# A two-layer decoder step on one core: gate and value of the feed-forward, for both row groups at once, from seven half-depth products in place of eight

## The chip, the cores and the metric

The kernel runs on one core of one Trainium2 chip. A core has a matrix engine (TensorE, PE in the profile, with its weight loads listed apart as PEld), three engines for element-wise work (VectorE or DVE, ScalarE or ACT, GpSimd or POOL), a queue engine that issues transfers (SP), an on-chip memory of 128 partitions (SBUF) and an accumulator memory of eight banks (PSUM). The metric is the device time of one execution in microseconds (us). Three timed runs of the kernel before gave 1133.88, 1135.64 and 1136.44 us; the median is 1135.64 us.

## What is computed

One inference step of a two-layer decoder on 520 rows of 1024 features: a new sequence of 512 rows ("prompt") and eight single rows of other sequences ("sample"). Layer 0 mixes tokens by windowed attention, layer 1 by gated linear attention; each is followed by a layer normalisation, a gated feed-forward with a causal convolution of width 3, and another normalisation. The change concerns the feed-forward. Cut to what matters, the reference has:

```python
def conv_ffn(x, buf, w_up, conv_w, conv_b, w_down):
    T = x.shape[1]
    h = x @ w_up
    a, u = h[..., :D_FF], h[..., D_FF:]
    ap = jnp.concatenate([buf.astype(a.dtype), a], axis=1)
    c = conv_b + sum(conv_w[j] * ap[:, j:j + T] for j in range(CONV_W))
    y = (jax.nn.gelu(c, approximate=False) * u) @ w_down
    return y, ap[:, T:]
...
        xp = layer_norm(ALPHA * xp + mp, ln_mix_g[i], ln_mix_b[i])
...
        fp, cp = conv_ffn(xp, buf0, ffn_w_up[i], ffn_conv_w[i], ffn_conv_b[i], ffn_w_down[i])
...
        xp = layer_norm(ALPHA * xp + fp, ln_ffn_g[i], ln_ffn_b[i])
```

D_FF is 2816, that is 22 blocks of 128 inner features; a is called the gate and u the value. All arrays are 32-bit floats.

## The kernel before

**Rows and groups.** Activations lie transposed: features on the 128 partitions, rows along the free axis. The 520 rows are cut into group a (prompt rows 0 to 255) and group b (prompt rows 256 to 511 and the 8 sample rows, 264 in all).

**A product in three passes.** TensorE multiplies numbers of type fp32r, which hold fewer bits than a 32-bit float. So each operand is kept as a pair: a rounded part ("h": `wh` of weights, `xh` of activations) and the rest ("l": `wl`, `xl`), and a product is the sum of three passes, wh·xh, wh·xl and wl·xh (lines 198, 200 and 202). `split` makes the pairs: ScalarE rounds (line 228, for weights 167), VectorE subtracts the rounded part from the original (line 229, for weights 170). A unit of work is one 128x1024 block of weights: one 512 KB transfer into a `raw` tile, one split, and one product of 8 depth steps for each group. Where both parts of group a's activations stand side by side (`xs_a`, `hs_a`), `product2` runs wh against both in one matmul of 512 columns and wl against one of 256 (lines 221 and 222); the two halves of the result are added afterwards.

**The feed-forward.** For inner block j there are two units, gate and value. `ffn_gate` copies the gate from PSUM into `aext` (line 637), forms the convolution into `conv` (lines 642 to 644; 648 for sample rows) and applies the Gelu (line 653). `ffn_value` multiplies (line 665) and splits the result into `hh` and `hl`. The 22 blocks come in three parts of 6, 8 and 8; after each part, eight units of the down-projection (`ffn_down`) add their share to the residual `x`. From block 4 on (`WIDE`), and in the first two parts of the down-projection, group a's products have the 512-column form.

**What sets the order.** `order` lists the products: group b follows group a some four or five units behind. Code that belongs later is put off by a number of products (`spawn`, `resume`, `due`). A scheduler then places each engine's instructions; the engines run them strictly in that order and wait for one another through semaphores. Six buffers hold split weights (`wts`), and a seventh (`wx`, `EXTRA`) during the feed-forward; as group b leaves a unit, the next one not yet loaded is started. `raw` has two buffers, the accumulators `accp` four banks.

**Before the feed-forward.** `ln_end` finishes the normalisation of each group: it writes `xh` and `xl`, and later adds a bias to `x` on GpSimd, one block at a time (line 361).

Of the kernel before, what the change touches and what calls it, by code (L numbers as in the profile page):

```python
# [46 lines left out]
EXTRA = 1  # L47
XEND = 8
# [12 lines left out]

WIDE = 4
# [35 lines left out]
class Net:  # L98
# [109 lines left out]
    def product2(self, g, u, rs, rh, rl, wide):  # L208


        if rs is None or not wide:
            return self.product(g, u, rh, rl), None
        nc = self.nc
        h, l = self.w[u]
        nt = self.units[u][1]
        ps = self.acc.tile([P, 512], F32, name="accp")
        o = ps.rearrange("p (j t) -> p j t", t=2)
        for k in range(nt):
            ks = slice(k * P, (k + 1) * P)
            last = k == nt - 1  # L220
            both = lambda: nc.tensor.matmul(o, h[:, ks], in_turn(rs[:, k].rearrange("p t q j -> p t (q j)")), start=k == 0, stop=last)  # L221
            low = lambda: nc.tensor.matmul(o[:, :P], l[:, ks], in_turn(rh[:, k]), start=False, stop=False)  # L222
            for f in (low, both) if last else (both, low):
                f()
        return ps[:, :256], ps[:, 256:]
# [59 lines left out]
    def ln_end(self, g, i, last=False):  # L285
# [319 lines left out]
    def ffn_open(self, layer):  # L605
        nc = self.nc
        if EXTRA:
            self.wx, self.wx_cm = self.open(f"wts{layer}", EXTRA)
# [10 lines left out]
        t = p.tile([P, NF, NS], F32, name="baset")  # L619
# [37 lines left out]
    def ffn_value(self, g, u, layer, j, q):  # L657
        nc, n = self.nc, g.n
        ps, lo = self.product2(g, u, g.xs, g.xh, g.xl, j >= WIDE)
        h = self.fp.tile([P, NT - 256], F32, name="hprod", bufs=2)  # L660
        if lo is not None:
            nc.scalar.copy(h[:, :n], lo)
            nc.vector.tensor_tensor(h[:, :n], h[:, :n], ps, op=ALU.add)
            ps = h[:, :n]
        nc.vector.tensor_tensor(h[:, :n], g.gate[:, :n], ps, op=ALU.mult)
# [507 lines left out]
```

## Time and profile before

| | value |
|---|---|
| timed, three runs (us) | 1133.88, 1135.64, 1136.44 |
| profiled execution, span (us) | 1131.7 |
| PE busy (us, share of the span) | 1104.2, 98% |
| PEld busy | 1055.1, 93% |
| DVE busy | 777.2, 69% |
| ACT busy | 565.7, 50% |
| POOL busy | 319.3, 28% |
| instructions on PE, DVE, ACT, POOL | 8806, 1626, 1251, 591 |
| read from main memory, written | 108.67 MB, 8.47 MB |

The span is the profiled execution's own time from its first to its last instruction; the timed runs lie 2.2 to 4.7 us above it. Busy times overlap, since engines work side by side. Matmuls are pipelined: the row of one shows about 280 ns, though the next starts 112 ns later, so the pace of a product is read from start to start. In a row of the profile, "out<-in" names the tiles written and read, "x6" counts instructions, and what follows "<-" in brackets is what the engine had waited for.

### The profile page before, as it was taken

Reading aid. Unit: us, or ns where it says so; the run is one execution under the profiler, and the core shown is the slowest. Engines: PE = TensorE matmul, PEld = TensorE weight load, DVE = VectorE, ACT = ScalarE, POOL = GpSimd, SP = SyncE. Lnnn points to the kernel's source line nnn. Section 1 sums busy time; section 2 is a strip of 40 time slices with the busy share of each in tenths; the row PEclk is TensorE's granted clock in tenths of the full one; section 3 lists DMA queues with packets and bytes.
Section 4 is the critical chain, followed back from the end, with each engine's and each line's share of the span. In section 5 each row is a group of like instructions: output and inputs, shape, how many; then the busy total and the mean of one; then the engine's idle time right before and its main releaser. Section 6 shows DMA issues by size and latency. Waiting matters only on the chain.

```text
span 1131.7 us, 22912 instructions
## 1 busy us (share of the span) xinstructions
PE 1104.2 (98%) x8806; PEld 1055.1 (93%) x8806; DVE 777.2 (69%) x1626; ACT 565.7 (50%) x1251; POOL 319.3 (28%) x591
## 2 busy tenths in 40 slices
PE   8999999999999999999999999999999999999996
PEld 7997799999999999999899999899999999999995
DVE  7897579655665566568867778779756665566565
ACT  5677556534553245435455556456524553245433
POOL 4575574400110011255211100374400110001243
PEclk9999999999999999999899999999999999999998
DMA  7553023333233233242124354432333223223222
GB/s 244 150 178 96 16 75 101 105 103 121 94 105 102 93 100 106 75 134 94 57 90 145 122 178 160 139 111 94 113 98 127 94 98 109 93 96 110 76 64 76
DMA packets 53804, 122.81 MB, mean 109 GB/s; under 512 B 6808, under 2 KB 27328, under 8 KB 53696
## 3 DMA queue, kind: packets, MB, share of 16 engines
q1 hardware_dynamic: 51536, 119.47, 32.8%
q10 hardware_dynamic: 2160, 1.89, 0.5%
q8 instruction: 69, 1.13, 0.4%
q14 instruction: 39, 0.32, 0.1%
HBM read 108.67 MB, written 8.47 MB: 104 GB/s over the span
## 4 chain that ended last, share of the span: by engine, by line
PE 77%; DVE 10%; DMA 5%; ACT 3%; issue 2%; POOL 1%; SPq 0%; ACTq 0%; DVEq 0%; POOLq 0%
PE accp L198 16%; PE accp L200 16%; PE accp L202 16%; PE accp L221 15%; PE accp L222 8%; DMA vb<-dv 2%; DVE xs_a L355 1%; DVE wl L183 1%; DVE wl L170 1%; DMA raw<-in_w_up 1%; DMA qs<-hl 1%; DVE sgla L910 1%; DVE x_a L353 1%; PE pv L554 1%; ACT pr L523 1%
## 5 line engine op out<-in xcount | busy, mean ns | idle before, releaser
L170 DVE TENSOR_TENSOR wl<-raw,wh 128x1024 fp32r<-128x1024 f32 (+2 forms) x172 | 207.0, 1205 | 103.3 <-ACT wh L167 102.7
L198 PE MATMUL accp<-xh_b,wh 128*128 128x264 f32 x976 | 272.5, 279 | 1.8 <-ACT xh_b L354 1.7
L167 ACT ACTIVATE wh<-raw 128x1024 fp32r<-128x1024 f32 (+2 forms) x168 | 173.6, 1033 | 199.8 <-PE accp L200 187.3
L202 PE MATMUL accp<-xh_b,wl 128*128 128x264 f32 x976 | 270.8, 277 | 0.0
L200 PE MATMUL accp<-xl_b,wh 128*128 128x264 f32 x960 | 266.5, 278 | 0.0
L221 PE MATMUL accp<-xs_a,wh 128*128 128x512 f32 x576 | 196.3, 382 | 0.0
L198 PEld LDWEIGHTS accp<-xh_b,wh 128*128 128x128 f32 x976 | 184.8, 189 | 3.3 <-ACT xh_b L354 2.3
L202 PEld LDWEIGHTS accp<-xh_b,wl 128*128 128x128 f32 x976 | 184.5, 189 | 0.8 <-issue 0.6
L200 PEld LDWEIGHTS accp<-xl_b,wh 128*128 128x128 f32 x960 | 181.6, 189 | 2.5 <-issue 0.4
L222 PE MATMUL accp<-xs_a,wl 128*128 128x256 f32 x576 | 145.4, 273 | 0.0
L198 PE MATMUL accp<-hh_b,wh 128*128 128x264 f32 x480 | 134.2, 280 | 1.7 <-ACT hh_b L228 1.1
L200 PE MATMUL accp<-hl_b,wh 128*128 128x264 f32 x480 | 134.6, 280 | 0.3 <-DVE hl_b L594 0.2
L202 PE MATMUL accp<-hh_b,wl 128*128 128x264 f32 x480 | 133.6, 278 | 0.0
L221 PEld LDWEIGHTS accp<-xs_a,wh 128*128 128x128 f32 x576 | 109.1, 189 | 11.4
L222 PEld LDWEIGHTS accp<-xs_a,wl 128*128 128x128 f32 x576 | 110.2, 191 | 1.9
L198 PE MATMUL accp<-xs_a,wh 128*128 128x256 f32 x400 | 107.6, 284 | 1.4 <-ACT wh L167 0.6
L200 PE MATMUL accp<-xs_a,wh 128*128 128x256 f32 x384 | 103.0, 282 | 0.6 <-DVE xs_a L229 0.3
L198 PEld LDWEIGHTS accp<-hh_b,wh 128*128 128x128 f32 x480 | 91.6, 191 | 2.3 <-ACT hh_b L228 1.6
L200 PEld LDWEIGHTS accp<-hl_b,wh 128*128 128x128 f32 x480 | 91.5, 191 | 1.8 <-DVE hl_b L594 0.4
L202 PEld LDWEIGHTS accp<-hh_b,wl 128*128 128x128 f32 x480 | 91.5, 191 | 0.2
L232 POOL COPY hist<-aext 128x2 f32<-128x2 f32 x44 | 10.2, 231 | 283.7 <-DVE aext L641 277.2
L198 PEld LDWEIGHTS accp<-xs_a,wh 128*128 128x128 f32 x400 | 77.2, 194 | 2.8 <-ACT wh L167 1.0
(338 smaller groups left out, 2505.5 us busy)
## 6 DMA issues: line engine op xcount, KB each, us to landing
raw<-in_w_up SPq DMA_DIRECT2D x88, 512.0 KB, 3.4
raw<-in_w_down SPq DMA_DIRECT2D x32, 512.0 KB, 3.4
raw<-in_w_gla SPq DMA_DIRECT2D x24, 512.0 KB, 3.4
raw<-in_w_mix_o SPq DMA_DIRECT2D x16, 512.0 KB, 4.1
raw<-in_w_down SPq DMA_DIRECT2D x16, 384.0 KB, 3.0
qs<-hl SPq DMA_DIRECT2D x64, 64.0 KB, 2.2
sgla<-in_state_gla SPq DMA_DIRECT2D x16, 256.0 KB, 2.7
vb<-dv SPq DMA_DIRECT2D x16, 256.0 KB, 3.7
```

The lines of the kernel that those rows point to most:

```text
L167: nc.scalar.activation(h[:, c], r[:, c], AF.Copy)
L170: nc.vector.tensor_tensor(l[:, c], r[:, c], h[:, c].bitcast(F32), op=ALU.subtract)
L183: self.nc.vector.tensor_tensor(l, r, h.bitcast(F32), op=ALU.subtract)
L198: nc.tensor.matmul(o, h[:, ks], xh, start=k == 0, stop=False)
L200: nc.tensor.matmul(o, h[:, ks], xl, start=False, stop=False)
L202: nc.tensor.matmul(o, l[:, ks], xh, start=False, stop=not tail and k == nt - 1)
L221: both = lambda: nc.tensor.matmul(o, h[:, ks], in_turn(rs[:, k].rearrange("p t q j -> p t (q j)")), start=k == 0, stop=last)
L222: low = lambda: nc.tensor.matmul(o[:, :P], l[:, ks], in_turn(rh[:, k]), start=False, stop=False)
L353: v = nc.vector.scalar_tensor_tensor(x[:, m], x[:, m], sc(m), rp, op0=ALU.mult, op1=ALU.mult)
L355: xl = nc.vector.scalar_tensor_tensor(g.xl[:, m], parted(x[:, m]), bi(m), g.xh[:, m].bitcast(F32), op0=ALU.add, op1=ALU.subtract)
L523: nc.scalar.activation(pr[:, b, 0:P + 1], sc[:, b, 0:P + 1], AF.Exp, bias=nm[:, b:b + 1], accum_out=den[:, b:b + 1])
L554: mm = nc.tensor.matmul(pv[64 * v:64 * v + 64, b * P:(b + 1) * P], self.vtok[:, kb, 64 * v:64 * v + 64], parts[v][w][:, b], start=i == 0, ...
```

## The change

From block j = 4 on (`PAIRED`), gate and value are one unit, a pair of weight blocks (`ffn_pair`). Cut the depth of 1024 into a lower and an upper half: the gate's weights become A11 and A12, the value's A21 and A22, the rows' halves B11 and B21 for group a and B12 and B22 for group b. The four results, gate and value for a and for b, are a product of two 2x2 block matrices, eight half-depth products. Winograd's form of Strassen's algorithm needs seven, at the price of sums: of weights (s1 to s4, four additions for each pair), of rows (t1 to t4, once in each layer) and of results.

- `load_pair` fetches two blocks, adds s1 to s4 on GpSimd, and splits seven half-blocks (as three tiles of 1024 columns and one of 512) where two units had four.
- `row_sums`, called by `ln_end`, makes t1 to t4 on GpSimd; `row_sum1` writes the split of t1 over group b's `xh` and `xl` when the first pair begins.
- `half_product` is 4 depth steps of three matmuls with 256 or 264 columns. `ffn_pair` calls it seven times and combines the results on VectorE (lines 765, 768, 776, 778 and 781), ScalarE (763 and 772) and GpSimd (773 and 779). Convolution, Gelu and gate times value then run over both groups at once (lines 784 to 791).
- The 512-column form is gone everywhere, also from the first two parts of the down-projection, and so is the seventh weight buffer. A pair takes three of the six weight buffers (`COST`) and a smaller tile of its own for s4; a new pair is begun when three are free (`load_next`).
- In `order`, a pair comes once both groups are up to date, and in the first two parts of the down-projection group b follows two units behind (`DOWNLAG`).

The diff, cut to its core:

```diff
+    def load_pair(self, u):
+        nc, half = self.nc, KD * P // 2
+        src0, src1 = self.units[u][0]
+        r0 = self.raw.tile([P, KD * P], F32, name="raw")
+        r1 = self.pp.tile([P, KD * P], F32, name="raw1", bufs=2)
+        nc.sync.dma_start(out=r1, in_=src1)
+        nc.sync.dma_start(out=r0, in_=src0)
+        s = self.pp.tile([P, KD * P], F32, name="sums")
+        s4 = self.pp.tile([P, half], F32, name="sum4")
+        lo, hi = slice(0, half), slice(half, KD * P)
+        add = lambda o, x, y: nc.gpsimd.tensor_tensor(o, x, y, op=ALU.add)
+        add(s[:, lo], r1[:, lo], r1[:, hi])
+        add(s[:, hi], s[:, lo], r0[:, lo])
+        add(s4, s[:, hi], r0[:, hi])
+        add(r1[:, lo], r1[:, lo], r0[:, lo])
+        for src in (r0, s, s4, r1):
+            pool, name = (self.pp, "4") if src is s4 else (self.wts, "")
+            h, l = (pool.tile(list(src.shape), F32R, name=part + name) for part in ("wh", "wl"))
+            self.split(h, l, src)
...
+    def half_product(self, ps, w, x, n):
...
+        for k in range(KD // 2):
+            ks = slice(k * P, (k + 1) * P)
+            rh, rl = (in_turn(r[:, k, :, :n // 2]) for r in (xh, xl))
+            self.nc.tensor.matmul(o, h[:, ks], rh, start=k == 0, stop=False)
+            self.nc.tensor.matmul(o, h[:, ks], rl, start=False, stop=False)
+            self.nc.tensor.matmul(o, l[:, ks], rh, start=False, stop=k == KD // 2 - 1)
...
+    def row_sums(self, i):
...
+        for k in range(half):
+            tt(self.t1[k], a.x[:, k, 0:256], b.x[:, k, 0:256], ALU.subtract)
+        r2, r3 = (self.pp.tile([P, KD * P], F32, name="raw1", bufs=2) for _ in range(2))
+        for k in range(half):
+            self.shift(b, i, half + k)
+            tt(r2[:, 256 * k:256 * k + 256], b.x[:, half + k, 0:256], self.t1[k], ALU.add)
+        for k in range(half):
+            self.shift(b, i, k)
+        tt(wide(r3), rows(b, hi), rows(b, lo), ALU.subtract)
...
+        r4 = self.pp.tile([P, KD * P], F32, name="sums")
+        tt(wide(r4), wide(r2), rows(a, hi), ALU.subtract)
...
     def ffn_gate(self, g, u, layer, j, q):
-        ps, lo = self.product2(g, u, g.xs, g.xh, g.xl, j >= WIDE)
+        ps = self.product(g, u, g.xh, g.xl)
...
+    def ffn_pair(self, u, layer, j, q):
...
+        self.half_product(p1, W["a11"], part(a, lo), n)
+        v = t("v", bufs=2)
+        nc.gpsimd.memset(v[:, n:], 0.0)
+        nc.scalar.copy(v[:, :n], p1[:, :n])
+        self.half_product(p2, W["a12"], part(a, hi), n)
+        nc.vector.tensor_tensor(g[:, 2:2 + n], p2[:, :n], v[:, :n], op=ALU.add)
+        q6, p5 = bank(), bank()
+        self.half_product(q6, W["s2"], t2, m)
+        nc.vector.tensor_tensor(v, q6[:, :m], v, op=ALU.subtract)
+        self.half_product(p5, W["s1"], t1, m)
+        s5, h = t("s5"), t("hprod", NT)
+        y = h[:, n:]
+        nc.scalar.copy(s5, p5[:, :m])
+        nc.gpsimd.tensor_tensor(y, s5, v, op=ALU.subtract)
+        p3, p7, q4 = bank(), bank(), bank()
+        self.half_product(p3, W["s4"], part(b, hi), m)
+        nc.vector.tensor_tensor(g[:, 2 + n:], p3[:, :m], y, op=ALU.add)
+        self.half_product(p7, W["s3"], t3, m)
+        nc.vector.tensor_tensor(v, v, p7[:, :m], op=ALU.subtract)
+        nc.gpsimd.tensor_tensor(h[:, n:], v, s5, op=ALU.subtract)
+        self.half_product(q4, W["a22"], t4, n)
+        nc.vector.tensor_tensor(h[:, :n], v[:, :n], q4[:, :n], op=ALU.subtract)
...
+        nc.vector.tensor_tensor(h, c, h, op=ALU.mult)
+        self.split(a.hh[:, q], a.hl[:, q], parted(h[:, :n]))
+        self.split(b.hh[:, q], b.hl[:, q], parted(h[:, n:]))
...
     def ffn_down(self, g, u, layer, part, m):
-        ps, lo = self.product2(g, u, g.hs, g.hh, g.hl, part < 2)
+        ps = self.product(g, u, g.hh, g.hl)
...
+    def load_next(self):
+        while self.nu < len(self.units) and self.live + self.cost(self.nu) <= WSLOTS:
+            u = self.nu
+            self.nu += 1
+            self.live += self.cost(u)
```

**Inside a part, VectorE.** Before, the instructions of one block in the second part stand in this row; `aext`, `conv` and `hprod` are the gate, its convolution and the product with the value:

```order
L170 TENSOR_TENSOR wl<-raw,wh 128x1024
L648 SCALAR_TENSOR_TENSOR conv<-aext,par,base 128x8
L643 SCALAR_TENSOR_TENSOR conv<-aext,par,conv 128x256
L644 SCALAR_TENSOR_TENSOR conv<-aext,par,conv 128x256
L663 TENSOR_TENSOR hprod<-hprod,accp 128x256
L665 TENSOR_TENSOR hprod<-conv,hprod 128x256
L229 TENSOR_TENSOR hs_a<-hprod,hs_a 128x2x128
L665 TENSOR_TENSOR hprod<-conv,accp 128x264
```

Now the row reads as follows, from a pair's fifth product on to the next pair's third (`raw_4454` is the value's raw block, with s3 in it, of the pair after next; `raw` and `sums` are the gate's block and s1 with s2 of the pair behind that one):

```order
L776 TENSOR_TENSOR aext<-accp,hprod 128x264
L778 TENSOR_TENSOR v<-v,accp 128x264
L787 SCALAR_TENSOR_TENSOR conv<-aext,par,base 128x8
L781 TENSOR_TENSOR hprod<-v,accp 128x256
L251 TENSOR_TENSOR wl<-raw_4454,wh 128x1024
L785 SCALAR_TENSOR_TENSOR conv<-aext,par,conv 128x512
L786 SCALAR_TENSOR_TENSOR conv<-aext,par,conv 128x512
L251 TENSOR_TENSOR wl<-raw,wh 128x1024
L765 TENSOR_TENSOR aext<-accp,v 128x256
L791 TENSOR_TENSOR hprod<-conv,hprod 128x520
L768 TENSOR_TENSOR v<-accp,v 128x264
L251 TENSOR_TENSOR wl<-sums,wh 128x1024
```

Behind these follow the splits of `hprod` for a and b and that of `sum4` (512 columns), and the row begins anew. The result of a pair's last product (line 781), the next pair's first (765) and third (768) are now separated by weight splits of the pair to come.

**Inside a part, GpSimd.** Before, a block gave GpSimd only fills and copies of 2 or 8 columns:

```order
L634 MEMSET aext 128x2
L232 COPY nconv_p<-aext 128x2
L232 COPY nconv_s<-aext 128x8
L232 COPY aext<-hist 128x2
L232 COPY hist<-aext 128x2
```

Now each pair gives it these:

```order
L222 TENSOR_TENSOR sums<-raw_4599 128x512
L762 MEMSET v 128x8
L222 TENSOR_TENSOR sums<-sums,raw 128x512
L222 TENSOR_TENSOR raw_4599<-raw_4599,raw 128x512
L758 MEMSET aext 128x2
L773 TENSOR_TENSOR hprod<-s_4538,v 128x264
L222 TENSOR_TENSOR sum_4603<-sums,raw 128x512
L254 COPY nconv_p<-aext 128x2
L254 COPY nconv_s<-aext 128x8
L779 TENSOR_TENSOR hprod<-v,s_4538 128x264
```

Six two-operand instructions per pair are new, four of them 512 columns wide, and the fill of `aext` that a pair's line 765 waits for stands behind three of these.

**At the start of a feed-forward, GpSimd.** Before, the bias of the normalisation stands among small copies:

```order
L361 TENSOR_SCALAR x_b<-x_b,par 128x264
L232 COPY aext<-hist 128x2
L232 COPY hist<-aext 128x2
L361 TENSOR_SCALAR x_a<-x_a,par 128x256
L232 COPY nconv_p<-aext 128x2
```

Now the row sums stand between the biases, and the first two pairs' weight sums behind them (`raw_2793` and `raw_2794` hold t2 and t3, `sums` first t4, then s1 and s2):

```order
L399 TENSOR_TENSOR raw_2793<-x_b,msq 128x256
L391 TENSOR_SCALAR x_b<-x_b,par 128x264 x4
L399 TENSOR_TENSOR raw_2794<-x_b 128x1024
L399 TENSOR_TENSOR tsum<-x_b 128x32
L391 TENSOR_SCALAR x_a<-x_a,par 128x256 x4
L254 COPY hist<-aext 128x2
L399 TENSOR_TENSOR sums<-raw_2793,x_a 128x1024
L254 COPY aext<-hist 128x2
L254 COPY nconv_p<-aext 128x2
L254 COPY nconv_s<-aext 128x8
L222 TENSOR_TENSOR sums<-raw_3227 128x512
```

The first pair's sums begin only when t4 has been formed.

More of the change, by code (lines that the diff above doesn't have):

```diff
@@ L45 @@
 HIACT = 2
-EXTRA = 1
-XEND = 8
+PAIRED = 4
+COST = 3
+DOWNLAG = 2
 ACCS = 4
@@ L60 @@
 LOWS = 7
-WIDE = 4
 SPAUSE = 2
@@ L206, in product, with cost @@
         return ps[:, :g.n]
[L208 to L218, printed above, removed]
-            ks = slice(k * P, (k + 1) * P)
[L220 to L225, printed above, removed]
+    def cost(self, u):
+        return COST if isinstance(self.units[u][0], tuple) else 1
@@ L363, in load_x, with row_sum1 @@
+    def row_sum1(self):
+        nc, b, n = self.nc, self.groups[1], P
+        for k in range(KD // 2):
+            self.split(b.xh[:, k, :, :n], b.xl[:, k, :, :n], parted(self.t1[k]))
+        for r in (b.xh, b.xl):
+            r = r[:, 0:KD // 2, :, n:]
+            nc.gpsimd.tensor_scalar(r, r.bitcast(F32), -1.0, 0.0, op0=ALU.mult, op1=ALU.add)
     def load_x(self, i, m0, m1):
@@ L618, in ffn_open @@
         b = self.par[:, C_CB + layer * NF:C_CB + (layer + 1) * NF].unsqueeze(2).broadcast_to([P, NF, NS])
-        t = p.tile([P, NF, NS], F32, name="baset")
+        self.pp, self.pp_cm = self.open(f"pair{layer}")
+        s = lambda i: [P, KD // 2, 2, (256 + NS * (i < 2)) // 2]
+        self.th, self.tl = ([self.pp.tile(s(i), F32R, name=f"{n}{i}") for i in range(3)] for n in ("th", "tl"))
+        self.cp, self.cp_cm = self.open(f"chain{layer}")
+        t = self.cp.tile([P, NF, NS], F32, name="baset")
         g = nc.gpsimd
@@ L658, in ffn_value @@
         nc, n = self.nc, g.n
[L659 to L664, printed above, removed]
+        ps = self.product(g, u, g.xh, g.xl)
+        h = self.cp.tile([P, NT - 256], F32, name="hprod", bufs=2)
         nc.vector.tensor_tensor(h[:, :n], g.gate[:, :n], ps, op=ALU.mult)
@@ L1001, in order @@
             for u in range(p0, p1):
-                out.append((0, u))
+                pair = self.cost(u) > 1
                 lead = max(LAG, min(top, p0 + 2 * top - u))
@@ L1005, in order @@
                     lead = LAG - 1
[L1006 removed]
+                if pair:
+                    lead = 0
+                elif self.units[u][2] == self.ffn_down and self.units[u][3][1] < 2:
+                    lead = DOWNLAG
+                if not pair:
+                    out.append((0, u))
+                while b <= u - max(lead, 1):
                     out.append((1, b))
                     b += 1
+                if pair:
+                    out.append((2, u))
+                    b = u + 1
             out += [(1, u) for u in range(b, p1)]
         return out
[L1012 to L1025 removed]
+    def load_next(self):
+        while self.nu < len(self.units) and self.live + self.cost(self.nu) <= WSLOTS:
+            u = self.nu
+            self.nu += 1
+            self.live += self.cost(u)
+            late = self.units[u][1] and any(e < u < e + 6 for e in (*self.phases[2:4], *self.phases[5:6]))
+            self.load_unit(u, late=late)
     def run(self):
@@ L1039, in run @@
                 pre()
-                if pre != self.gla_open:
-                    for _ in range(EXTRA):
-                        self.next_unit(True)
-            self.slot += 1
-            self.resume(f(g, u, *a))
-            if i == 1:
-                x = self.extra.pop(u, False)
-                if not x or self.more(u):
-                    self.next_unit(x)
-                elif not self.extra:
-                    self.close_wx = True
-            if self.close_wx and self.fp is None:
-                self.close(self.wx_cm)
-                self.close_wx = False
+            self.slot += COST if i == 2 else 1
+            if i == 2:
+                f(u, *a)
+            else:
+                self.resume(f(self.groups[i], u, *a))
+            if i:
+                self.live -= self.cost(u)
+                self.load_next()
             self.due()
```

116 lines of the change are left out of this document (81 added, 35 removed).

## The prediction

> **What bounds the kernel now.** I read the page first: its sums, then the chain of work that ended last.
>
> ```profile
> span 1131.7 us, 22912 instructions
> PE 1104.2 (98%) x8806; PEld 1055.1 (93%) x8806; DVE 777.2 (69%) x1626; ACT 565.7 (50%) x1251; POOL 319.3 (28%) x591
> PE 77%; DVE 10%; DMA 5%; ACT 3%; issue 2%; POOL 1%; SPq 0%; ACTq 0%; DVEq 0%; POOLq 0%
> ```
>
> PE is busy 98% of the span and makes up 77% of the chain. Inside the stage that is changed it is fuller still. One inner block, in the busy times by stretch (columns: length, then PE, PEld, DVE, ACT and POOL busy with their instructions, granted clock, DMA):
>
> ```profile
> core 0: us, PE busy (x) PEld busy (x) DVE busy (x) ACT busy (x) POOL busy (x), PEclk, DMA share, GB/s
> 289.80:300.40 10.60, 10.60 (x82) 10.18 (x81) 6.82 (x14) 5.77 (x11) 1.29 (x5) 1.00 0.32 100
> ```
>
> So the stage is bound by the matrix engine at full clock, VectorE is two thirds full, and GpSimd has little to do. The pace of a product is read from start to start in the order of time on PE:
>
> ```profile
> 176.02 0.28 PE L198 MATMUL accp<-xs_a,wh 128*128 128x256 f32 x1
> ...
> 178.70 0.28 PE L198 MATMUL accp<-xs_a,wh 128*128 128x256 f32 x1
> ...
> 276.61 0.38 PE L221 MATMUL accp<-xs_a,wh 128*128 128x512 f32 x1
> ...
> 279.23 0.28 PE L198 MATMUL accp<-xh_b,wh 128*128 128x264 f32 x1
> ...
> 281.93 0.38 PE L221 MATMUL accp<-xs_a,wh 128*128 128x512 f32 x1
> ```
>
> A unit takes 2.62 us for group a in the 512-column form and 2.70 for b, 5.32 together; a block of two units 10.64. A plain product of a, the 24 matmuls from 176.02 to 178.70, takes 2.68.
>
> **PE's work.** Seven half-products replace four products: three of 256 columns (2.68 / 2 = 1.34) and four of 264 (1.35), 9.42 us. A pair saves 10.64 − 9.42 = 1.22 us, and 36 pairs (18 in each layer) 43.9. The down-projection loses the 512-column form in its first two parts: 14 depth steps x 8 units x 2 layers x (2.68 − 2.62) / 8 = +1.7. If PE stayed the bound, that would be nearly all.
>
> **VectorE's work for a pair.** Durations by form and by tile:
>
> ```profile
> L170 DVE TENSOR_TENSOR wl<-raw,wh 128x1024 fp32r<-128x1024 f32 x150 | 187.7, 1252 | 90.0 <-ACT wh L167 89.5 <-PE accp L202 0.3
> L391 DVE TENSOR_TENSOR wl<-raw,wh x2: 693/694/694, 4.3 to 7.8; 128x512 fp32r<-128x512 f32 x2
> L665 DVE TENSOR_TENSOR hprod<-conv,accp 128x264 f32<-128x264 f32 x44 | 18.9, 430 | 25.4 <-PE accp L202 25.3
> L229 DVE TENSOR_TENSOR hl_b<-hprod,hh_b 128x264 fp32r<-128x264 f32 x44 | 21.3, 485 | 1.2 <-ACT hh_b L228 1.2
> L648 DVE SCALAR_TENSOR_TENSOR conv<-aext,par,base 128x8 f32<-128x8 f32 x44 | 10.0, 227 | 0.1
> ```
>
> Weight splits: three of 1.25 and one of 512 columns, 0.69: 4.44. Five results from PSUM at 0.43: 2.15. Convolution: two of 512 columns, 0.73 each by the 0.69 row and its small surplus for a third operand (my estimate), and 0.23: 1.69. Gate times value over 520 columns: 0.70. Two splits at about 0.47: 0.94. Together 9.9 us against 6.8 before. VectorE alone would then be no faster than 9.9; instructions that follow without a wait start up to 0.1 early (169.55 + 0.48 against 169.96 below), so some 8.8 to 9.9. That is level with PE's 9.42.
>
> ScalarE rounds the same columns, 3.5 tiles at 1.06, and adds copies and activations of about 2.8, 6.5 us a pair. It is not the bound:
>
> ```profile
> L167 ACT ACTIVATE wh<-raw 128x1024 fp32r<-128x1024 f32 x150 | 158.8, 1059 | 169.2 <-PE accp L200 157.1 <-DMA raw<-in_w_mix_o 7.5 <-DMA raw<-in_w_up 1.5
> ```
>
> **What GpSimd does to VectorE.** This term decides. At the start of the first feed-forward both engines work at once; their rows in order of time, VectorE's first:
>
> ```profile
> 160.29 2.05 DVE L353 SCALAR_TENSOR_TENSOR x_a<-x_a,par,pv 128x256 f32<-128x256 f32 x5
> ...
> 169.55 0.48 DVE L355 SCALAR_TENSOR_TENSOR xs_a<-x_a,par,xs_a 128x256 fp32r<-128x256 f32 x1
> 169.96 1.75 DVE L183 TENSOR_TENSOR wl<-raw,wh 128x1024 fp32r<-128x1024 f32 x1
> 171.63 0.42 DVE L252 SCALAR_TENSOR_TENSOR x_b<-x_b,accp 128x264 f32<-128x264 f32 x1
> ```
>
> ```profile
> 157.35 4.18 POOL L306 TENSOR_TENSOR x_a<-x_a,mu 128x256 f32<-128x256 f32 x6
> 161.48 0.75 POOL L282 TENSOR_TENSOR s_b<-s_b,x_b 128x264 f32<-128x264 f32 x1
> ...
> 169.75 0.87 POOL L282 TENSOR_TENSOR s_b<-s_b,x_b 128x264 f32<-128x264 f32 x1 [1.99 <-DVE x_b L252]
> 170.59 1.73 POOL L283 TENSOR_TENSOR s_b<-s_b,sq 128x264 f32<-128x264 f32 x1
> ```
>
> The weight split at 169.96 takes 1.75 in place of 1.25, since GpSimd's addition runs until 170.62; GpSimd's next one, issued at 170.59, takes 1.73 in place of 0.75, since it waits for that split. The two take turns. The five instructions at 160.29 have one operand in PSUM and take their usual 0.41 each beside GpSimd's 0.75. So VectorE instructions with two SBUF operands exclude GpSimd's, and those with a PSUM operand do not.
>
> The Trainium skill ("SBUF — State Buffer", Who interferes with whom) says that the engines share a port pair which the first comer holds for its whole instruction; the rows agree up to 264 columns, and by this rule a 512-column addition shuts VectorE out to its end, which the low price in the second rival below would deny.
>
> How long does GpSimd hold it? Six of 256 columns take 4.18, 0.70 each; one of 176 takes 0.55:
>
> ```profile
> L623 POOL TENSOR_TENSOR base<-base,baset x2: 547/552/557, 144.0 to 751.0; 128x176 f32<-128x176 f32 x2
> L389 POOL TENSOR_SCALAR wh<-raw x2: 619/736/853, 3.7 to 6.9; 128x512 fp32r<-128x512 f32 x2
> ```
>
> (0.70 − 0.55) / 80 is 1.9 ns a column, so 512 columns with two operands cost 0.70 + 256 x 0.0019 = 1.2 us. Below stands the row with one operand, 0.74; above, twice 264 columns, 1.5. I take 1.25. A pair has four of these and two of 264 columns (0.72): 6.4 us, and 0.2 for two small copies: 6.6.
>
> VectorE's two-operand work holds the port for its columns alone, about (1.25 − 0.69) / 512 = 1.1 ns each: 3584 columns of splits, 1024 of convolution, 520 and 520: 5648 columns, 5.9 to 6.2 us. Port time per pair: 6.6 + 6.1 = 12.7. That exceeds 10.64 already. Walking one period in the order of the two engines, the port also stands idle: the fill of `aext` stands behind three additions, line 765 waits for it, and GpSimd then has nothing until line 768 gives `v`; lines 765, 768 and part of 776 and 778 pass with the port unused, about 1.1 us. A period of **13.8 us**, with PE waiting 4.4 in it, in two gaps of about 2 (banks free only once VectorE reaches lines 765, 768, 776 and 778). Bounds: 12.7 − 4 x 0.5 = 10.7 if the additions cost the one-operand row, 9.9 if they blocked nothing; above, every hold added to VectorE's 9.9, less 2.1 beside PSUM operands, 14.4, and with additions at 1.5, 15.4.
>
> **Which pairs pay it.** Two pairs' weights fit in the six buffers. In a part of eight pairs, six are computed while another pair is prepared; the last two have only down-projection blocks beside them. There, and for the two pairs in the first part, PE sets the pace, about 9.7. So 24 pairs of 36 take 13.8, and 12 take 9.7: 24 x (13.8 − 10.64) = +75.8 and 12 x (9.7 − 10.64) = −11.3.
>
> **Start of the feed-forward.** This stretch runs from the normalisation to block 4:
>
> ```profile
> 144.00:202.00 58.00, 56.98 (x492) 55.99 (x491) 48.10 (x89) 34.71 (x67) 34.92 (x50) 1.00 0.30 100
> ```
>
> Added on GpSimd: eight sums of 256 columns (5.6), two of 1024 (about 2.2 each), eight of 512 (10): 20 us on 34.9, so 55 of 58. Added on VectorE: the first two pairs' splits less the four units' they replace (8.9 − 5.0), those of t2 to t4 (3.8) and t1 (1.9): 9.6 on 48.1, so 57.7. With half of GpSimd's 20 in VectorE's way it is 68, 10 too late: **+10** in each layer, between 0 and 20. Total +20.
>
> **End of a part.** The last pair's gate and value for both groups become ready together. From its last result come gate times value, ScalarE's rounding and the subtraction, 0.7 + 0.5 + 0.5 with their waits some 3 us; the first down-projection product covers seven of its eight steps, 2.35. About 1 us each, six times: +6.
>
> Sum: 75.8 − 11.3 + 20 + 6 + 1.7 = **+92**. The profiled execution would be 1131.7 + 92 = 1224; the timed median lies 3.9 above the span, so **1228 us**. Transfers are no term: the same bytes at the 100 GB/s of the block above, over a longer stage.
>
> **Rivals.**
>
> 1. *PE stays the bound, the other engines fit in* (faster). VectorE's 8.8 to 9.9 lies beside 9.42, GpSimd's additions fall where VectorE has PSUM operands: −43.9 + 1.7 + 6, 1135.6 − 36 = **1099**; at VectorE's 9.9 for 24 pairs, −17.8 − 11.3 + 7.7, **1114**. It decides if GpSimd's holds cost VectorE under 0.9 us a pair. For it speaks PE's fullness and that ScalarE is free; against it the turns at 169.96. Chance 0.13.
>
> 2. *Port bound, but at its floor*: shorter holds, better packing, 12.6 a pair, the start 4 late. 24 x 1.96 − 11.3 + 8 + 4 + 1.7 = +49, **1185**. Chance 0.18.
>
> 3. *PE's gaps also cost clock.* In one place of this trace PE stood still for 2.6 us:
>
> ```profile
> 541.00:543.60 2.60, 0.02 (x2) 0.01 (x1) 2.60 (x9) 1.47 (x5) 0.00 (x0) 1.00 0.02 6
> 543.60:554.00 10.40, 10.32 (x35) 8.31 (x36) 7.81 (x21) 6.03 (x14) 0.00 (x0) 0.51 0.06 13
> ```
>
> The clock was then half for 10.4 us. Two gaps of 2 us in each period could do the same. Always at half, a pair would take 18.8; three quarters of the time, 9.42 / 0.625 = 15.1, so some 15.5 with the other waits: 24 x 4.86 − 11.3 + 20 + 7.7 = +133, **1269**. In the other periods the slack of 4.4 absorbs it. Chance 0.18.
>
> The Trainium skill ("TensorE: Matmul & The Clock Gate", Part 1) has the clock fall after an idle window of about 3.4 us, so gaps of 2 us would not do it and this rival would get no chance. The row above shows 2.6 us to be enough, and I go by the row.
>
> 4. *Nothing to be seen*: the steady pairs come out near 11, the gain of the other twelve making up for the rest. Chance 0.03.
>
> **How the numbers follow.** The forecast keeps 0.48. Faster by over 0.2% is rival 1, 0.13 less a little for its upper edge: 0.12. Within 0.2%, about what a measurement of this kernel can tell from no change, 0.03; slower 0.85. The range reaches over rival 2 and most of rival 3 and holds back rival 1 and the far end: 1150 to 1285.
>
> **What would show it.** In the profile after, right if: a pair in the middle of a part takes 13 to 15 us from one first product to the next; there VectorE's weight splits average 1.7 us or more and GpSimd's 512-column additions 2 us or more; PE's idle time names line 765, 768, 776 or 778 of VectorE as its releaser; the two last pairs of a part take under 10. Wrong if PE stays above 95% busy in the pairs, if the additions average under 1 us, or if the splits keep their 1.25. The start term shows as PE idle time ahead of the first pair of each layer, the clock rival as PEclk under 0.9 in the pairs' slices.

## The result, and the profile after

The changed kernel takes **1212.5 us** (median, 1212.1 to 1213.4) against 1135.3 for the kernel before on the same chip: 1.069 times as long, with a 95% interval of 1.067 to 1.070. Times are medians; one of the four executions of experiment 4, a slow one of 2824 us, is left out. The profiled execution took 1213.4 us with a span of 1211.5, 79.8 more than the 1131.7 before; the forecast was +92.

From the page of the changed kernel, its sums, the granted clock in 40 slices, and the chain that ended last:

```profile
span 1211.5 us, 24182 instructions
PE 1104.3 (91%) x9174; PEld 1063.1 (88%) x9174; DVE 957.2 (79%) x1684; ACT 598.3 (49%) x1233; POOL 614.9 (51%) x797
PEclk9999998899989999999899999998899899999898
PE 44%; DVE 28%; issue 8%; ACT 7%; POOL 6%; DMA 6%; SPq 0%; DVEq 0%; ACTq 0%; POOLq 0%
```

PE is as long busy as before although it has less to do (part of it at half clock), and its share of the chain fell from 77% to 44%, VectorE's rose from 10% to 28%. VectorE gained 180 us of busy time, GpSimd 296.

Where the 80 us lie is read from the busy times by stretch (columns as in the prediction). Of the first layer: four plain blocks, two pairs, down-projection, eight pairs, down-projection, eight pairs; of the second: the same start and the two runs of eight:

```profile
core 0: us, PE busy (x) PEld busy (x) DVE busy (x) ACT busy (x) POOL busy (x), PEclk, DMA share, GB/s
167.13:223.90 56.77, 50.21 (x391) 46.99 (x390) 48.65 (x73) 29.90 (x56) 46.07 (x56) 0.94 0.26 84
223.90:253.50 29.60, 22.59 (x171) 22.27 (x170) 25.52 (x41) 14.80 (x28) 15.42 (x24) 0.88 0.39 121
253.50:285.80 32.30, 32.30 (x291) 32.30 (x290) 19.61 (x30) 10.03 (x12) 10.64 (x10) 1.00 0.27 87
285.80:380.70 94.90, 82.42 (x675) 80.60 (x674) 86.64 (x111) 48.16 (x75) 58.37 (x67) 0.95 0.31 100
...
423.70:517.50 93.80, 79.98 (x675) 77.95 (x674) 86.51 (x110) 48.21 (x75) 55.58 (x65) 0.98 0.26 86
...
799.90:859.20 59.30, 51.93 (x391) 48.94 (x391) 49.48 (x78) 30.68 (x57) 48.06 (x59) 0.91 0.28 91
859.20:887.60 28.40, 21.96 (x170) 21.64 (x169) 23.55 (x38) 14.63 (x27) 13.28 (x21) 0.88 0.33 109
...
919.90:1014.80 94.90, 82.67 (x674) 80.80 (x673) 86.23 (x110) 48.11 (x75) 58.33 (x67) 0.95 0.30 100
1058.00:1153.50 95.50, 82.10 (x675) 80.56 (x674) 86.94 (x111) 47.99 (x75) 55.51 (x65) 0.95 0.26 83
```

The same stretch at the start of the kernel before holds 4 x 10.76 + 2 x 10.64 = 64.3 us of products, with PE standing still for 1.0:

```profile
167.00:231.30 64.30, 63.28 (x512) 61.23 (x511) 51.35 (x101) 36.15 (x73) 25.87 (x51) 1.00 0.33 105
```

In the start PE also works at a lowered clock, which the kernel before does not (1.00 above). Two pieces of it:

```profile
195.00:202.00 7.00, 5.77 (x36) 5.77 (x37) 3.70 (x6) 3.12 (x6) 7.00 (x12) 0.66 0.24 76
...
237.00:244.00 7.00, 7.00 (x48) 7.00 (x49) 4.91 (x10) 3.21 (x6) 2.59 (x7) 0.76 0.58 187
```

In the second PE has no gap and gets through 48 matmuls, where 7 us at full clock hold 65 (216 to 223).

Put against the prediction's terms (a run of eight blocks before: 8 x 10.64 = 85.1):

| term | forecast | measured |
|---|---|---|
| four runs of eight pairs | 24 x 3.16 − 8 x 0.94 = +68 | 379.1 − 340.5 = +39 |
| start and the two pairs behind it, both layers | +20 − 4 x 0.94 = +16 | 174.1 − 128.6 = +45 |
| ends of parts, down-projections | +6 + 1.7 = +8 | the rest, −4 |
| sum | +92 | +80 |

So two errors of about 30 us, of opposite sign, hide in a total that is off by 12: that the total came so close is luck.

**A steady period.** VectorE in order of time, from one line 778 to the next:

```profile
308.21 0.42 DVE L778 TENSOR_TENSOR v<-v,accp 128x264 f32<-128x264 f32 x1
308.54 0.53 DVE L787 SCALAR_TENSOR_TENSOR conv<-aext,par,base 128x8 f32<-128x8 f32 x1
...
309.33 1.77 DVE L251 TENSOR_TENSOR wl<-raw,wh 128x1024 fp32r<-128x1024 f32 x1
311.02 1.76 DVE L785 SCALAR_TENSOR_TENSOR conv<-aext,par,conv 128x512 f32<-128x512 f32 x1
312.82 1.64 DVE L786 SCALAR_TENSOR_TENSOR conv<-aext,par,conv 128x512 f32<-128x512 f32 x1
314.38 2.28 DVE L251 TENSOR_TENSOR wl<-raw,wh 128x1024 fp32r<-128x1024 f32 x1
316.59 0.41 DVE L765 TENSOR_TENSOR aext<-accp,v 128x256 f32<-128x256 f32 x1
...
321.03 0.43 DVE L776 TENSOR_TENSOR aext<-accp,hprod 128x264 f32<-128x264 f32 x1 [0.65 <-POOL hprod L773]
321.38 0.42 DVE L778 TENSOR_TENSOR v<-v,accp 128x264 f32<-128x264 f32 x1
```

and GpSimd in the same time:

```profile
307.78 1.27 POOL L222 TENSOR_TENSOR sum<-sums,raw 128x512 f32<-128x512 f32 x1
...
309.26 0.76 POOL L779 TENSOR_TENSOR hprod<-v,s 128x264 f32<-128x264 f32 x1
309.98 2.26 POOL L222 TENSOR_TENSOR sums<-raw 128x512 f32<-128x512 f32 x1
...
312.31 1.60 POOL L222 TENSOR_TENSOR sums<-sums,raw 128x512 f32<-128x512 f32 x1
313.88 1.71 POOL L222 TENSOR_TENSOR raw<-raw,raw 128x512 f32<-128x512 f32 x1
```

The period is 13.17 us. The sum at 307.78 lies beside lines 776 and 778, which have a PSUM operand: it takes 1.27 and costs VectorE only 0.3 us, in line 787 (0.53 in place of 0.23). What follows takes turns with VectorE. The split at 309.33 takes 1.77, since GpSimd's line 779 runs until 310.02. The sum at 309.98 waits for that split, which ends at 311.10, then runs to 312.24; line 785, issued at 311.02, ends 0.54 behind it; 312.31 waits for line 785 (312.78) and runs to 313.91, line 786 ends 0.55 behind it; and so on. Line 765, which frees a PSUM bank, comes only then, and PE's waits name it. In the whole period VectorE is busy for 12.5 of the 13.17 us, and for the other 0.65 it waits, ahead of line 776, for GpSimd's line 773. The largest waits of PE (engine, line, releaser: us in total, times, longest):

```profile
PE accp L245 <- DVE aext L765: 42.2, 17, 3.1
PE accp L245 <- DVE hprod L737: 13.4, 4, 4.5
PE accp L198 <- ACT wh L167: 8.1, 6, 2.3
PE accp L245 <- DVE aext L776: 7.5, 16, 1.3
```

The groups of instructions by form, for comparison with the experiments (xcount | busy us, mean ns | idle before):

```profile
L251 DVE TENSOR_TENSOR wl<-raw,wh 128x1024 fp32r<-128x1024 f32 x72 | 129.1, 1794 | 12.2 <-ACT wh L250 12.2
L785 DVE SCALAR_TENSOR_TENSOR conv<-aext,par,conv 128x512 f32<-128x512 f32 x36 | 47.7, 1326 | 0.7 <-ACT conv L784 0.7
L222 POOL TENSOR_TENSOR sums<-raw 128x512 f32<-128x512 f32 x36 | 65.9, 1832 | 54.7 <-issue 26.5 <-DVE wl L251 24.5 <-DVE tl L251 3.5
```

### The profile page after: what moved, and what is told of

Its sections match the earlier page's. It is cut to its first block, busy times and chain, and to the rows that moved or that the text cites. A ratio compares the mean times of both kernels' runs of the same rounds, so it can differ in the third digit from the quotient of the medians.

```text
span 1211.5 us, 24182 instructions
## 1 busy us (share of the span) xinstructions
PE 1104.3 (91%) x9174; PEld 1063.1 (88%) x9174; DVE 957.2 (79%) x1684; ACT 598.3 (49%) x1233; POOL 614.9 (51%) x797
## 4 chain that ended last, share of the span: by engine, by line
PE 44%; DVE 28%; issue 8%; ACT 7%; POOL 6%; DMA 6%; SPq 0%; DVEq 0%; ACTq 0%; POOLq 0%
PE accp L200 9%; PE accp L198 9%; PE accp L202 9%; DVE wl L251 4%; PE accp L245 4%; PE accp L246 3%; PE accp L247 3%; DVE conv L786 3%; DVE conv L785 3%; DMA vb<-dv 2%; ACT wh L250 2%; POOL hprod L773 2%; ACT conv L790 1%; DVE wl L170 1%; DMA raw<-in_w_qkv 1%
## 5 line engine op out<-in xcount | busy, mean ns | idle before, releaser
L245 PE MATMUL accp<-th,wh 128*128 128x264 f32 (+1 forms) x432 | 128.5, 297 | 44.4 <-DVE aext L765 42.2
L170 DVE TENSOR_TENSOR wl<-raw,wh 128x1024 fp32r<-128x1024 f32 (+3 forms) x102 | 124.8, 1227 | 22.6 <-ACT wh L167 22.0
L251 DVE TENSOR_TENSOR wl<-raw,wh 128x1024 fp32r<-128x1024 f32 x72 | 129.1, 1794 | 12.2 <-ACT wh L250 12.2
L200 PE MATMUL accp<-hs_a,wh 128*128 128x256 f32 x480 | 131.3, 277 | 0.6 <-DVE hs_a L251 0.6
L202 PE MATMUL accp<-hs_a,wl 128*128 128x256 f32 x480 | 130.8, 276 | 0.0
L198 PE MATMUL accp<-hs_a,wh 128*128 128x256 f32 x480 | 129.5, 278 | 0.1
L246 PE MATMUL accp<-tl,wh 128*128 128x264 f32 (+1 forms) x432 | 126.1, 292 | 0.0
L247 PE MATMUL accp<-th,wl 128*128 128x264 f32 (+1 forms) x432 | 125.9, 291 | 0.0
L198 PE MATMUL accp<-xh_b,wh 128*128 128x264 f32 x400 | 115.0, 287 | 3.5 <-ACT xh_b L376 3.5
L202 PE MATMUL accp<-xh_b,wl 128*128 128x264 f32 x400 | 113.0, 282 | 0.0
L200 PE MATMUL accp<-xl_b,wh 128*128 128x264 f32 x384 | 107.8, 281 | 0.0
```

The lines of the kernel that those rows point to most:

```text
L170: nc.vector.tensor_tensor(l[:, c], r[:, c], h[:, c].bitcast(F32), op=ALU.subtract)
L198: nc.tensor.matmul(o, h[:, ks], xh, start=k == 0, stop=False)
L200: nc.tensor.matmul(o, h[:, ks], xl, start=False, stop=False)
L202: nc.tensor.matmul(o, l[:, ks], xh, start=False, stop=not tail and k == nt - 1)
L245: self.nc.tensor.matmul(o, h[:, ks], rh, start=k == 0, stop=False)
L246: self.nc.tensor.matmul(o, h[:, ks], rl, start=False, stop=False)
```

## The experiments

Theory: GpSimd's sums and VectorE's instructions with two SBUF operands take turns; VectorE's lengthened period holds PE's banks. Rivals: A, VectorE is full by its own added work; B, GpSimd's own queue is the cause; C, the four PSUM banks; D, PE's lost clock. Where not said otherwise an edit is made to the changed kernel.

**1. The sums left out.** The splits read raw weights; all other work stays.

```diff
-        add(s[:, lo], r1[:, lo], r1[:, hi])
...
-        for src in (r0, s, s4, r1):
+        for i, src in enumerate((r0, r1, r1[:, lo], r1)):
```

> Leaves out the four sums of weights per pair; the splits read the raw weights in their place, so ScalarE and VectorE do the same number of instructions of the same shapes. Theory (the sums on GpSimd and VectorE's instructions with two SBUF operands take turns): VectorE's 1024-column splits go back to about 1.25 us, the two 512-column conv steps to about 0.73; the steady pair falls from 13.18 us to PE's pace, 9.5 to 10.2; about 20 periods x (13.18 - 9.9) = 66 us less, and some 6 us less in each layer's start: 1135 us, between 1120 and 1155. Rival A (VectorE is full by its own added work): splits stay near 1.8, 1205 to 1215 us. Rival B (GpSimd's own queue delays the aext fill and line 773): also faster, but with the splits' mean hardly moved.

Measured: 1124.5 us, 0.992 of the kernel before (0.990 to 0.993). Busy times of a period from line 772 (778 above) to the next, then one form:

```profile
315.69:325.40 9.71, 9.69 (x87) 9.53 (x85) 9.03 (x16) 6.38 (x10) 2.41 (x6) 1.00 0.32 111
```

```profile
L779 DVE SCALAR_TENSOR_TENSOR conv<-aext,par,conv 128x512 f32<-128x512 f32 x36 | 28.3, 786 | 0.1
```

The period is 9.71, PE full at full clock, VectorE busy for 9.03; the conv step is back at 0.79. Rival A falls: VectorE's own work fits beside PE's. The four sums cost 13.17 − 9.71 = 3.46 us a pair, and VectorE's busy time falls by as much, from 12.5 to 9.03. The edit also takes away the splits' wait for the sums; experiment 3 keeps it.

**2. The sums done twice.**

```diff
         add(s[:, hi], s[:, lo], r0[:, lo])
+        add(s[:, lo], r1[:, lo], r1[:, hi])
...
```

> Each of the four sums' work is done twice (eight 512-column additions per pair; the result is unchanged). Theory: 4 x 1.27 = 5.1 us more port time per pair, all of it on VectorE's period: 13.18 -> about 18 in the runs of eight, 20 x 5 = 100 us more, and 5 to 10 more in each start: 1320 us, between 1290 and 1340. Rival A (VectorE full by its own work; GpSimd 51 per cent busy has room): under 15 us more, 1212 to 1228.

Measured: 1312.1 us (1310.2 to 1314.0), ratio 1.157 (1.153 to 1.160). 100 us more, as the theory said, but not in its way: lines 782 (778 above) follow one another in the first run of eight at 12.8 to 16.7 us, not 18. GpSimd was busy for 66% of the span, but for 16.4 of the 16.7 us of such a period, waiting for its turn included. So this run does not tell the turns from rival B; the next one does.

**3. The convolution in PSUM.**

```diff
-        c = t("conv", NT)
+        c, e = self.mtile("sc"), t("tail", NS)
```

> The convolution's accumulator is in a PSUM bank in place of SBUF, so VectorE's two 512-column conv steps and the 512-column gate product have one SBUF operand each; GpSimd's sums and all counts stay, but for two more small instructions of 8 columns. Theory: these three steps cost their own 0.7 us beside GpSimd's sums (conv steps' mean 1.3 -> 0.75), port time falls by 3 x 0.56 = 1.7 us, the steady pair goes from 13.18 to about 11.4: 36 us less, 1176 us, between 1165 and 1192. Rival A (VectorE's own work): the same number of columns, so 1208 to 1218. Rival B (GpSimd's queue): its instructions are the same, 1205 to 1215.

Measured: 1174.0 us, ratio 1.035 (1.033 to 1.038). By form:

```profile
L785 DVE SCALAR_TENSOR_TENSOR sc<-aext,par,sc 128x512 f32<-128x512 f32 x36 | 26.8, 744 | 0.5 <-ACT sc L784 0.5
L251 DVE TENSOR_TENSOR wl<-raw,wh 128x1024 fp32r<-128x1024 f32 x72 | 126.2, 1753 | 11.2 <-ACT wh L250 11.2
```

The conv step takes 0.74, in place of 1.33, with GpSimd's sums still there, while the splits, still with two SBUF operands, keep their 1.75. In the trace lines 778 follow one another every 11.14 us. GpSimd's instructions are the same as before, so rival B does not explain these 38 us. This is the fastest of the kernels here that compute everything with the pairs, and it is still 39 us slower than the kernel before.

**4. The sums on VectorE itself.**

```diff
-        add = lambda o, x, y: nc.gpsimd.tensor_tensor(o, x, y, op=ALU.add)
+        add = lambda o, x, y: nc.vector.tensor_tensor(o, x, y, op=ALU.add)
```

> The four sums of a pair on VectorE in place of GpSimd; nothing else changes. Theory (the sums on GpSimd cost VectorE 13.18 - 9.71 = 3.47 us a pair as it is): four 512-column instructions with two SBUF operands at VectorE's own 0.69 are 2.8 us, so VectorE needs some 12.4 to 12.9 a pair and the time is the same or a little less: 1195 to 1212 us. If GpSimd's sums were mostly free beside VectorE's work, the move would add 2 us or more a pair: 1250 us or more.

Measured: 1187.3 us, ratio 1.046 (1.044 to 1.049): 25 us *less* than with GpSimd, more than I had allowed. By form:

```profile
L222 DVE TENSOR_TENSOR sums<-raw 128x512 f32<-128x512 f32 x36 | 26.4, 733 | 0.3
L251 DVE TENSOR_TENSOR wl<-raw,wh 128x1024 fp32r<-128x1024 f32 x72 | 92.9, 1290 | 5.8 <-ACT wh L250 5.8
```

The four sums take VectorE about 4 x 0.71 = 2.8 us when it makes them; made by GpSimd they lengthen its period by 3.46. The first run of eight takes 91.2 us in place of 94.9.

**5. Two sums on VectorE, and the convolution in PSUM.**

```diff
+        nc.vector.tensor_tensor(s[:, lo], r1[:, lo], r1[:, hi], op=ALU.add)
...
+        nc.vector.tensor_tensor(r1[:, lo], r1[:, lo], r0[:, lo], op=ALU.add)
```

> The convolution in PSUM and two of the four sums (s1 and s3) on VectorE, the other two on GpSimd. VectorE's own work becomes about 9.9 + 0.2 + 1.4 = 11.5 us a pair, GpSimd's holds fall to 4.0, which fit beside VectorE's 4.3 us with a PSUM operand. Theory: steady pair 10.9 to 11.6, about the same as with all four on GpSimd (11.14): 1168 to 1186 us.

Measured: 1184.7 us, ratio 1.044 (1.042 to 1.047), inside the expected bounds at their upper end; the mixture is worse than all four sums on GpSimd with the convolution in PSUM. The period is not as expected: in the middle of the first run lines 778 follow at 11.5 to 14.8 us in place of 10.9 to 11.6. The cause is not traced.

**6. Copies in place of sums.**

```diff
-        add = lambda o, x, y: nc.gpsimd.tensor_tensor(o, x, y, op=ALU.add)
+        add = lambda o, x, y: nc.gpsimd.tensor_copy(o, y)
```

> Each of a pair's four sums on GpSimd becomes a copy of 512 columns with one operand (the addition is left out; count, places, buffers and waits stay). If GpSimd's instructions shut VectorE out for their length whatever their operands (a one-operand instruction of 512 columns took 0.74 in the kernel before, the sum 1.27): holds of 3.0 in place of 5.1 us a pair, steady pair 13.18 -> 11 to 12, 1165 to 1185 us. If only two-operand instructions exclude each other: conv steps at 0.75, splits at 1.25, steady pair 9.7 to 9.9 as without sums, 1124 to 1136 us.

Measured: 1173.8 us, ratio 1.034 (1.032 to 1.036). GpSimd in order of time:

```profile
303.92 1.60 POOL L222 COPY sum<-raw 128x512 f32<-128x512 f32 x1
...
309.95 0.61 POOL L222 COPY raw<-raw 128x512 f32<-128x512 f32 x1 [0.32 <-DMA raw<-in_w_up]
```

A copy alone takes 0.61; the one at 303.92 waits for a weight split of VectorE that ends at 305.05. So an instruction with one operand takes turns as well, only for half as long; the time stands between no sums and sums. Without the chain from sum to sum the scheduler also put the instructions in another order, so the 38.7 us are not the price of the second operand alone.

**7. Six banks for a pair's products.**

```diff
-        p3, p7, q4 = bank(), bank(), bank()
+        p3, p7, q4 = bank(), self.mtile("sc"), self.mtile("sc")
```

> The last two of a pair's seven products go to two PSUM banks of their own, so a pair has six banks in place of four. Theory (VectorE's 13.18 us a pair sets the pace, and PE's waits for banks only follow from it): steady pairs stay at 13.1 to 13.3, 1203 to 1217 us. Rival C (four banks tie PE and VectorE together): steady pairs fall by 1 us or more, 1192 us or less.

Measured: 1205.5 us, ratio 1.061 (1.059 to 1.063); lines 778 still follow at 13.15 to 13.24 in the first run of eight. The kernel is 70 us above the one before on the same chip, the changed one 77, so two more banks are worth some 8 us and rival C is not the cause.

**8. Matmuls that fill PE's gap.**

```diff
+        if j >= 6 and 1 <= q <= 5:
+            f = self.mtile("tp")
+            for _ in range(2):
+                self.half_product(f, W["a11"], part(a, lo), n)
```

> 24 matmuls without use (2.6 us at full clock, into a bank of their own) ahead of the third product of pairs 2 to 6 of each run of eight, where PE stands still for 3.1 us; the fall of the clock to half after these gaps should go with the gaps. Theory (VectorE's period of 13.2 sets the pace, PE's lost clock lies in its slack): runs of eight stay at 93 to 96 us, granted clock in them 0.98 to 1.00 in place of 0.95, total 1206 to 1220 us. Rival (the lost clock costs time): runs of eight fall by 4 us or more each, total 1180 to 1198 us.

Measured: 1233.8 us, ratio 1.087 (1.084 to 1.090). The first run of eight:

```profile
287.40:387.54 100.14, 90.76 (x795) 89.37 (x793) 89.94 (x112) 47.04 (x75) 61.79 (x67) 1.00 0.30 95
```

The clock came back to 1.00 and the run became 5.2 us longer, so the lost clock was not what cost the time. But neither theory gave this number: the 2.6 us of filler lengthened the period by 1.0, so PE seems not to be free of the loop (bank, product, VectorE, bank), and the test does not price the clock by itself. The changed kernel does that better, with three of its periods from line 778 to line 778:

```profile
308.21:321.39 13.18, 9.87 (x84) 9.57 (x84) 12.50 (x17) 6.33 (x10) 8.90 (x11) 1.00 0.28 81
321.39:334.54 13.15, 9.87 (x68) 9.71 (x68) 12.47 (x17) 5.29 (x10) 8.90 (x11) 0.80 0.27 81
334.54:347.91 13.37, 12.54 (x103) 12.20 (x101) 11.69 (x17) 7.38 (x11) 8.55 (x11) 0.94 0.26 80
```

At a clock of 0.80 the period is 13.15, at 1.00 it is 13.18: the loss lies in PE's slack, but for 0.2 in the third, where VectorE's line 781 waits 0.50 for PE. Rival D falls for the runs of eight. For the start, where PE works at a lowered clock too, no run tests it.

**9. No pairs in the first part** (`PAIRED = 6` in place of 4).

> The first part's two pairs become plain blocks (32 pairs of 44 blocks instead of 36 in both layers), so the first pairs' weights are prepared beside down-projections. If the start's loss (22 us a layer against the kernel before) comes from preparing and starting pairs beside the row sums: 14 to 18 us less a layer, 1180 us, between 1176 and 1190. If it comes from the row sums alone (56.8 us for four plain blocks that need 43.0), the two blocks cost 21.3 in place of 29.6 and the rest stays: 1196. If the first pairs' entry cost only moves to the next part: 1205 to 1212.

Measured: 1206.1 us, ratio 1.063 (1.060 to 1.066). 6 us, as the third expectation had it, but not for its reason: the runs of eight are unchanged (94.8 us for the first). From the first product of the layer to the first run of eight it takes 112.5 in place of 118.7 us; the kernel before has 64.3 + 32.3 = 96.6 us of work there. Of the 16 us between, PE is idle for 6.2 and busy 9.7 longer with the same products, at a granted clock of 0.54 from 188 to 195 and 0.50 from 195 to 202. So most of the start's loss is there without any pair near it. The next two runs look for its cause.

**10. The kernel before without its seventh weight buffer** (`EXTRA = 0` in place of 1).

> The kernel before with its seventh weight buffer of the feed-forward taken away (EXTRA = 0), which the change also took away; no pairs, no sums. In the changed kernel PE has only group b's 24 products between 185.9 and 193.99, which wait for x_b, and then waits for a weight split, where the kernel before has group a's products of a further unit to put between them. If the missing buffer makes the start's loss: 8 to 17 us in each layer, 1151 to 1170 us. If GpSimd's row sums make it: 1134 to 1141 us.

Measured: 1150.6 us, ratio 1.014 (1.012 to 1.016): 8 us a layer, without any pair or sum, at the lower edge of the first expectation. PE's waits from 166 to 210 in the kernel before, and without the buffer:

```profile
PE accp L198 <- ACT xh_b L354: 0.9, 1, 0.9
```

```profile
PE accp L198 <- ACT wh L167: 2.2, 1, 2.2
PE accp L198 <- ACT xh_b L354: 1.9, 2, 1.3
```

While group b's first product waits for the eight pieces of x_b, the kernel before puts group a's next products between them; without the buffer their weights are not there yet. These waits make 3.2 of the 8 us. From 167 to 202 PE gets through 224 matmuls in place of 291, at a granted clock of 0.95 in place of 1.00, so a part of the price may be lost clock.

**11. No row sums on GpSimd.** Left out are the sums t1 to t4 of rows of x; the splits read rows of x.

```diff
-            tt(self.t1[k], a.x[:, k, 0:256], b.x[:, k, 0:256], ALU.subtract)
...
-        for q, r in enumerate((r2, r3, r4)):
+        for q, r in enumerate((rows(b, lo), rows(b, hi), rows(a, hi))):
```

> The changed kernel without the row sums on GpSimd (t1 to t4: eight 256-column sums, two of 1024 and one small, left out; the splits read rows of x in their place, the same columns). If GpSimd's row sums make the start's loss of 22 us a layer: 12 to 20 us less a layer, 1172 to 1190 us. If the missing seventh buffer makes it: 1200 to 1210 us. The runs of eight pairs stay at 94 to 95.5 us in both.

Measured: 1200.0 us, ratio 1.058 (1.055 to 1.060). Start and two pairs take 79.4 and 80.0 us in the two layers in place of 86.4 and 87.7: 7 to 8 a layer, less than the first expectation and as the second had it. The edit also leaves the buffers `raw1` and `sums` free for the first pairs' weights, so these 7 to 8 us are the row sums with the buffers that they hold.

In experiment 1, without the pairs' sums, this stretch takes 76.8 and 78.4: 9 to 10 less. With the 8 of the buffer the three make 24 to 26 us a layer where 22 to 23 are lost: added up they account for the start and overlap a little. That the buffer is worth the same in the changed kernel is assumed, not shown, and the three amounts contain what PE loses by the lowered clock.

**12. Two sums by DMA** (from the kernel of experiment 3). s1 and s3 are made by accumulating transfers.

```diff
-        add(s[:, lo], r1[:, lo], r1[:, hi])
+        nc.sync.dma_start(out=s[:, lo], in_=src1[:, lo])
+        nc.gpsimd.dma_start(out=s[:, lo], in_=src1[:, hi], accum_op=ALU.add)
...
-        add(r1[:, lo], r1[:, lo], r0[:, lo])
+        nc.gpsimd.dma_start(out=r1[:, lo], in_=src0[:, lo], accum_op=ALU.add)
```

> The kernel with the convolution in PSUM, and two of the four weight sums (s1 and s3) made by an accumulating DMA in place of GpSimd; the other two stay on GpSimd. Theory (port time): 2 x 1.27 = 2.5 us less a pair on the port, 11.14 -> PE's 9.5 to 10 if the issue of the two DMAs and their landing cost GpSimd little: run of eight 76 to 80 us in place of 85, total 1136 to 1158 us. If the accumulating DMAs land too late or their issue holds GpSimd as long as the sums did: 1174 us or more.

Measured: 1251.6 us, ratio 1.103 (1.100 to 1.105), 78 us above experiment 3: the second expectation came true, far beyond its 1174. Median us from issue to landing, per transfer:

```profile
sums<-in_w_up SPq DMA_DIRECT2D x36, 256.0 KB, 3.4
sums<-in_w_up POOLq DMA_DIRECT2D x36, 256.0 KB, 4.4
```

GpSimd, which issues the accumulating transfers, waits for transfers into `sums` in order, ahead of its other work: 13.5 us from 300 to 370, and VectorE waits 12.6 us there for GpSimd's line 774 (773 above). In the first run of eight VectorE is busy for 75.4 of 102.4 us, where the changed kernel has 86.6 of 94.9: less time goes into turns, and waiting took its place. A second `sums` buffer was not tried.

## Why the prediction was right, and where it was not

- **Mechanism.** Right: the period is VectorE's, lengthened by GpSimd's sums, and PE waits for line 765. Runs 1 and 3 move the time with the sums and with VectorE's second SBUF operand, and run 6 with the length of GpSimd's instructions. The Trainium skill ("SBUF — State Buffer", Who interferes with whom) has VectorE instructions with two SBUF inputs, and not those with one, contend with GpSimd's reads; the conv step's 1.33 and 0.74 us, before and after its accumulator left SBUF, agree.
- **VectorE's work alone**, 8.8 to 9.9 us a pair: 9.03 busy in run 1. Right.
- **The 512-column sum**, 1.25 us estimated: 1.27 alone. Right.
- **The period**, 13.8: it is 13.17. The walk let line 765 wait for the fill of `aext` behind three additions; in the trace the fill is done before VectorE gets there. What makes it is 9.03 of VectorE's own work, 3.47 by turns and 0.65 of waiting for line 773; PE's gaps in it are one of 3.1 and one of 0.2, not two of 2. The bounds of 9.9 to 15.4 held it.
- **"24 steady pairs".** This step failed by count. In a run of eight the distances of lines 778 are five of about 13.2, one of 10.2 to 11.5 and one of 10.2 to 10.6, and the first pair pays nothing: its products take 9.4 us. With the period's 0.6 this makes +39 where +68 was forecast.
- **The start**, "+10 in each layer": this step failed most; start and two pairs lose 22 to 23. I counted only work on VectorE and GpSimd. Of that kind are the pairs' sums (9 to 10) and the row sums (7 to 8). The seventh weight buffer, which the change removes, had no term at all: 8 us a layer in the kernel before. And I let the two pairs of the first part run at PE's pace of 9.7; the two take 29.6 and 28.4, in the first layer with PE waiting 4.5 and 2.5 us for line 737 of VectorE. Nor did any term allow for the lowered clock in the start; its share is open.
- **End of a part**, +6: nothing. The down-projections begin without a wait (PE 32.30 of 32.30). The rest of −4 I have not traced to a cause.
- **The signs.** Two did not come as written: GpSimd's 512-column additions average 1.4 to 1.8 us by form, not 2, and the splits 1.79 for the two raw blocks but 1.27 for `sums`.
- **Rival 1** (PE bound, 1099 to 1114) is what the sums' absence nearly gives: 1124.5 with the start's other losses still in. **Rival 2** (1185) had the period at 12.6. **Rival 3**: the clock did fall to half behind gaps of 3.1 us, though not behind each, and in the runs of eight it cost next to nothing. The matmuls of 264 columns start every 0.11 us ahead of the gap and every 0.22 behind it:

```profile
326.85 0.28 PE L246 MATMUL accp<-xl_b,wh 128*128 128x264 f32 x1
326.97 0.28 PE L247 MATMUL accp<-xh_b,wl 128*128 128x264 f32 x1
330.32 0.56 PE L245 MATMUL accp<-th,wh 128*128 128x264 f32 x1 [3.08 <-DVE aext L765]
330.68 0.43 PE L246 MATMUL accp<-tl,wh 128*128 128x264 f32 x1
330.90 0.43 PE L247 MATMUL accp<-th,wl 128*128 128x264 f32 x1
```

The Trainium skill ("TensorE: Matmul & The Clock Gate", Part 1) puts the fall behind an idle window of about 3.4 us; here 3.08 was enough, and the measurement decides. An equal gap, of 3.08 up to 317.15, was not followed by a fall (granted clock 1.00 until 321).

## What to carry to other kernels

Before arithmetic is moved to an idle GpSimd to save TensorE time, ask how much of its duration VectorE will lose in the stage where it lands: here four sums of 1.27 us cost VectorE 3.46 us a pair, more than the 2.8 of making them itself, and the 1.2 us saved on TensorE were lost almost three times over. Moving an operand from SBUF to PSUM took the conv steps out of that contest, 0.74 in place of 1.33 us each. And a buffer that a change drops has a price of its own: look at what it fills in the trace before it goes.

## What was not expected of the hardware

A GpSimd instruction with one operand took turns with VectorE as well (the copy of 0.61 us took 1.60 beside a weight split). A 256 KB accumulating transfer issued from GpSimd landed after 4.4 us, against 3.4 for a plain one.
